# Seven more q, k and v weight chunks as three fp32r products instead of one plain fp32 product

## The chip, the cores and the metric

The kernel runs on one core of a Trainium2 chip. The metric is the device time of one execution in microseconds (us). A run of the comparison gives the median of several executions. One execution was also profiled: its rows are what the prediction rests on.

## The reference

One decoder layer over 256 tokens and 1024 channels, all in float32. A conditioning vector c gives six vectors of shift, scale and gate (adaLN). The first half of the layer is a token mixer with two groups that share one input projection:

```python
h = rms_norm(x, norm1_g) * (1 + scale1) + shift1
q, k, v, z, xbc, dt = split(h @ w_in)          # 1024, 1024, 1024, 1024, 1536, 16 columns
y_attn = rms_norm(causal_attention(rms_norm(q), rms_norm(k), v), attn_norm_g)   # 8 heads of 128
y_ssm  = group_rms_norm((ssd(silu(conv4(xbc)), dt) + x_ssm * d_skip) * silu(z), ssm_norm_g)
x = x + gate1 * (concat(y_attn, y_ssm) @ w_out)
```

The second half is a causal ConvFFN of width 2816 with its own norm, shift, scale and gate2. With 256 tokens the block-sparse attention is causal attention over one block.

## The kernel before

Weights come from memory as **chunks** of 128 partitions by up to 1024 columns, 512 KB, in one fixed order: 17 chunks of a first stage (the x, B, C, dt and a part of the z columns of the input projection), and then, counted from 0, chunks 0 to 4 (the rest of z), 5 to 20 (q and k), 21 to 28 (v), 29 to 44 (the output projection) and the FFN's. This second count is the one that the change and all texts here use. Chunks 24 and 28 have 512 columns.

Each chunk is loaded into a ring of 8 raw buffers by the loader's queue (SP, line 146), which runs in order and also issues the loads of the adaLN weight tiles (line 152, a ring of 3) and of the decay rows (line 558). A raw load waits until the chunk that used the buffer eight chunks before has given it back. A chunk is then used in one of two ways:

- **plain**: its matmuls read the raw buffer in float32, and the buffer is given back after the last of them.
- **split**: ScalarE rounds it to a hi part (line 189; GpSimd at line 187 for a few), VectorE subtracts to get the lo part (line 191), the raw buffer is given back, and every product is done as three fp32r matmuls: hi by hi, lo by hi, hi by lo, with the activations split in the same way. The hi and lo buffers are rings of five. Splits are written two chunks ahead of their use.

Which chunks are plain is a list:

```python
def plain(i):
    return i - N1 in PLAIN
...
                    if plain(c):
                        pe.matmul(bs[t], h32[:, kt, blk(t)], w[:, wc], start=(q4 == k2 == 0), stop=(kt == KT - 1))   # L806
                        continue
                    pe.matmul(bs[t], hhi[:, kt, blk(t)], w[0][:, wc], start=(q4 == k2 == 0), stop=False)   # L808
                    pe.matmul(bs[t], hhi[:, kt, blk(t)], w[1][:, wc], start=False, stop=False)             # L809
                    pe.matmul(bs[t], hlo[:, kt, blk(t)], w[0][:, wc], start=False, stop=(kt == KT - 1))    # L810
```

Between the chunks of q, k and v a table of units places other work: the convolution and softplus of the SSM group, its decay matrices (ScalarE at lines 564 to 570, VectorE at 568 to 571, products on TensorE at 582), the adaLN sums (VectorE at line 239; for one tile of this stage GpSimd at 244 with ScalarE at 248), the squares, Newton steps (lines 281 to 287), scaling (line 642) and transposes (line 648) of q and k, and then attention's scores, softmax, transposes and products. The order of each engine's instructions from the second stage on is set by a planner when the kernel is built, from the order in which they are written and from its own costs; only the loader's queue keeps the written order.

Of the kernel before, what the change touches and what calls it, by code (L numbers as in the profile page):

```python
# [21 lines left out]
NF = D_FF // 128  # L22
EPS = 1e-6
LAG = 2
PLAIN = [0, 1, 2, 3, 4, 5, 6, 8, 10, 12, 14, 16, 18, 20, 22, 24, 26, 28, 29, 30, 31, 32, 33, 34, 35, 36, 45, 46]
NEG = -1.0e30
SCALE = 128.0 ** -0.5

# [19 lines left out]
def mixer_ffn(ctx: ExitStack, tc: tile.TileContext, xT_d, c_d, vec_d, alog_d, ada_d,  # L48
# [120 lines left out]
    def plain(i):  # L169

        return i - N1 in PLAIN

# [862 lines left out]
```

## Time and profile before

| | |
|---|---|
| time, median of 3 runs | 452.51 us (451.82 to 453.27) |
| the profiled execution's own time | 452.11 us |
| its span, first to last instruction | 450.4 us |
| mean granted TensorE clock | 0.984 |
| TensorE, VectorE, ScalarE, GpSimd busy | 96%, 76%, 58%, 14% of the span |
| memory traffic | 96.71 MB, mean 215 GB/s |

The span leaves 1.7 us of the execution's time outside. PE is TensorE's matmuls and PEld its weight loads, which run beside them; DVE is VectorE, ACT ScalarE, POOL GpSimd and SPq the loader's queue. Times in rows are us from the start of the span unless they are marked ns. The granted clock is given as a share of the full clock.

### The profile page before, as it was taken

What the parts mean: (1) busy time and instruction counts of PE and PEld (TensorE: products, weight loads), DVE (VectorE), ACT (ScalarE), POOL (GpSimd) and SP (SyncE); (2) the same over time, 40 slices, a digit from 0 to 9 for tenths busy, and PEclk for the clock granted to TensorE, in tenths of its full rate; (3) what the DMA queues carried; (4) which work ended last, traced back from release to release, by engine and by line L of the source; (5) the groups of instructions that cost most, each with busy time, mean ns of one, the idle gap of its engine ahead of it and who ended that gap; (6) DMA issues with size and microseconds to landing.
All of it is one profiled execution on the core that took longest, in us unless ns stands there. A gap on an engine that the chain in (4) does not pass through costs nothing.

```text
span 450.4 us, 7730 instructions
## 1 busy us (share of the span) xinstructions
PE 433.8 (96%) x2900; PEld 384.7 (85%) x2900; DVE 344.4 (76%) x666; ACT 259.3 (58%) x523; POOL 62.3 (14%) x46
## 2 busy tenths in 40 slices
PE   7977999999999999999999989999999999999996
PEld 7876999867665566788899879999999999999996
DVE  4999992999567998647889478877777887777764
ACT  4535582945497668543237448566666665555540
POOL 3576400000000020100220000023322300000000
PEclk9789899999999999999999999999999999999999
DMA  7999674777558654245695073878677755654002
GB/s 287 399 402 400 203 239 149 255 283 268 175 175 283 229 207 182 94 141 188 222 412 206 20 307 110 282 246 258 228 254 260 234 185 186 193 174 156 0 1 95
DMA packets 31029, 96.71 MB, mean 215 GB/s; under 512 B 3712, under 2 KB 6672, under 8 KB 30992
## 3 DMA queue, kind: packets, MB, share of 16 engines
q1 hardware_dynamic: 30960, 96.20, 61.0%
q8 instruction: 23, 0.38, 0.4%
q14 instruction: 14, 0.11, 0.1%
q10 hardware_dynamic: 32, 0.02, 0.0%
HBM read 95.14 MB, written 1.06 MB: 214 GB/s over the span
## 4 chain that ended last, share of the span: by engine, by line
PE 73%; DMA 13%; DVE 7%; ACT 4%; SPq 1%; issue 1%; POOL 1%; DVEq 0%
PE bank L336 17%; PE bank L338 17%; PE bank L337 17%; PE bank L834 6%; DMA ada<-in_ada_dram 5%; PE bank L806 5%; PE bank L785 4%; DMA adax<-in_ada_dram 2%; DMA raw<-in_wv_dram 2%; DMA raw<-in_win_dram 2%; PE bank L906 1%; DVE wlo L191 1%; DMA xT<-in_xT_dram 1%; DVE ada L239 1%; DMA raw<-in_winq_dram 1%; DMA ab<-acd 1%
## 5 line engine op out<-in xcount | busy, mean ns | idle before, releaser
L191 DVE TENSOR_TENSOR wlo<-raw,whi 128x1024 fp32r<-128x1024 f32 (+3 forms) x112 | 137.4, 1235 | 15.4 <-ACT whi L189 15.0
L189 ACT ACTIVATE whi<-raw 128x1024 fp32r<-128x1024 f32 (+3 forms) x111 | 104.3, 953 | 36.7 <-PE bank L338 21.7
L336 PE MATMUL bank<-h2hi,whi 128*128 128x256 f32 x336 | 95.4, 285 | 2.1 <-ACT h2hi L876 1.9
L337 PE MATMUL bank<-h2hi,wlo 128*128 128x256 f32 x336 | 94.5, 283 | 0.0
L338 PE MATMUL bank<-h2lo,whi 128*128 128x256 f32 x336 | 93.9, 284 | 0.0
L336 PEld LDWEIGHTS bank<-h2hi,whi 128*128 128x128 f32 x336 | 64.4, 192 | 3.7 <-ACT h2hi L876 3.2
L244 POOL TENSOR_TENSOR ada<-ada,cb 128x1024 f32<-128x1024 f32 x13 | 33.4, 2569 | 241.8 <-DMA ada<-in_ada_dram 241.8
L337 PEld LDWEIGHTS bank<-h2hi,wlo 128*128 128x128 f32 x336 | 64.4, 192 | 0.0
L892 DVE SCALAR_TENSOR_TENSOR fbuf<-bank,vec,fbuf 128x255 f32<-128x255 f32 x84 | 40.4, 482 | 30.9 <-ACT fbuf L890 29.6
L338 PEld LDWEIGHTS bank<-h2lo,whi 128*128 128x128 f32 x336 | 63.8, 192 | 0.2 <-DVE h2lo L877 0.2
L336 PE MATMUL bank<-fsp,whi 128*128 128x256 f32 x176 | 49.8, 284 | 0.0
L337 PE MATMUL bank<-fsp,wlo 128*128 128x256 f32 x176 | 49.7, 283 | 0.0
L338 PE MATMUL bank<-fsp,whi 128*128 128x256 f32 x176 | 49.6, 283 | 0.0
L890 ACT ACTIVATE fbuf<-bank,vec 128x256 f32<-128x256 f32 x42 | 23.5, 561 | 36.4 <-PE bank L338 36.4
L806 PE MATMUL bank<-raw,h 128*128 128x512 f32 x96 | 44.3, 595 | 0.0
L336 PE MATMUL bank<-hhi,whi 128*128 128x256 f32 (+1 forms) x128 | 37.9, 296 | 3.7 <-DVE vS L409 2.4
L337 PE MATMUL bank<-hhi,wlo 128*128 128x256 f32 (+1 forms) x128 | 38.0, 297 | 2.2 <-DVE wlo L191 2.2
L338 PE MATMUL bank<-hlo,whi 128*128 128x256 f32 (+1 forms) x128 | 37.8, 295 | 0.7 <-DVE hlo L386 0.7
L336 PEld LDWEIGHTS bank<-fsp,whi 128*128 128x128 f32 x176 | 33.8, 192 | 0.1
L337 PEld LDWEIGHTS bank<-fsp,wlo 128*128 128x128 f32 x176 | 33.8, 192 | 0.0
L338 PEld LDWEIGHTS bank<-fsp,whi 128*128 128x128 f32 x176 | 33.7, 192 | 0.0
L239 DVE SCALAR_TENSOR_TENSOR ada<-ada,cb 128x1024 f32<-128x1024 f32 x25 | 30.3, 1216 | 3.5 <-DMA ada<-in_ada_dram 3.5
(222 smaller groups left out, 828.2 us busy)
## 6 DMA issues: line engine op xcount, KB each, us to landing
raw<-in_wup_dram SPq DMA_DIRECT2D x44, 512.0 KB, 4.2
ada<-in_ada_dram SPq DMA_DIRECT2D x38, 512.0 KB, 5.0
raw<-in_wdn_dram SPq DMA_DIRECT2D x22, 512.0 KB, 3.5
raw<-in_winq_dram SPq DMA_DIRECT2D x16, 512.0 KB, 4.3
raw<-in_wout_dram SPq DMA_DIRECT2D x16, 512.0 KB, 3.8
adax<-in_ada_dram SPq DMA_DIRECT2D x10, 512.0 KB, 7.6
raw<-in_win_dram SPq DMA_DIRECT2D x18, 256.0 KB, 7.0
raw<-in_winv_dram SPq DMA_DIRECT2D x6, 512.0 KB, 6.0
```

Of the source, the lines that this page charges most:

```text
L189: act.activation(hi[:, c], t[:, c], AF.Copy)
L191: (pool if lo_on_pool(i) else dve).tensor_tensor(lo[:, c], t[:, c], hi[:, c].bitcast(F32), op=OP.subtract)
L239: dve.scalar_tensor_tensor(t, t, 1.0, sc, op0=OP.mult, op1=OP.mult, accum_out=mod[:, i:i + 1])
L244: pool.tensor_tensor(adas[i], adas[i], sc, op=OP.mult)
L336: pe.matmul(out, w[0], h[0], start=start, stop=False, skip_group_check=True)
L337: pe.matmul(out, w[1], h[0], start=False, stop=False, skip_group_check=True)
L338: pe.matmul(out, w[0], h[1], start=False, stop=stop, skip_group_check=True)
L785: pe.matmul(zo[i], w[:, blk(kt)], h32[:, kt, 0:S], start=(kt == 0), stop=(kt == KT - 1), skip_group_check=True)
L806: pe.matmul(bs[t], h32[:, kt, blk(t)], w[:, wc], start=(q4 == k2 == 0), stop=(kt == KT - 1))
L834: pe.matmul(sacc(d), w[:, blk(kt)], X["y32"][:, kt], start=(kt == d % 2 == 0), stop=(kt == 7), skip_group_check=True)
L890: act.activation(a, src, AF.Identity, bias=vec[:, V_FB + i:V_FB + i + 1], scale=vec[:, w + 2:w + 3])
L892: dve.scalar_tensor_tensor(a[:, s:], src[:, :S - s], vec[:, w + 2 - s:w + 3 - s], a[:, s:], op0=OP.mult, op1=OP.add)
```

## The change

The list of plain chunks loses 8, 10, 12, 16, 18, 26 and 28. These seven chunks (two halves of q, two of k and the second half of v; chunk 28 is the one of 512 columns) are from then on split and done in three fp32r products. Plain remain 0 to 6, 14, 20, 22, 24, 29 to 36, 45 and 46.

```diff
-PLAIN = [0, 1, 2, 3, 4, 5, 6, 8, 10, 12, 14, 16, 18, 20, 22, 24, 26, 28, 29, 30, 31, 32, 33, 34, 35, 36, 45, 46]
+PLAIN = [0, 1, 2, 3, 4, 5, 6, 14, 20, 22, 24, 29, 30, 31, 32, 33, 34, 35, 36, 45, 46]
```

## Rows read from the trace of the kernel before

**Rows 1.** The page, part 1: engine, busy us, share of the span, instructions.

```profile
PE 433.8 (96%) x2900; PEld 384.7 (85%) x2900; DVE 344.4 (76%) x666; ACT 259.3 (58%) x523; POOL 62.3 (14%) x46
```

**Rows 2.** Busy us of each engine by stretch, granted clock, DMA share, GB/s.

```profile
core 0: us, PE busy (x) PEld busy (x) DVE busy (x) ACT busy (x) POOL busy (x), PEclk, DMA share, GB/s
...
94.00:110.00 16.00, 16.00 (x58) 9.40 (x58) 14.66 (x34) 6.06 (x15) 0.00 (x0) 1.00 0.72 268
110.00:145.00 35.00, 34.99 (x154) 21.58 (x154) 22.00 (x48) 26.39 (x79) 0.00 (x0) 1.00 0.66 207
145.00:170.00 25.00, 25.00 (x111) 14.79 (x110) 24.14 (x75) 17.89 (x61) 2.93 (x1) 1.00 0.65 232
170.00:194.50 24.50, 23.80 (x116) 17.67 (x116) 17.90 (x66) 15.89 (x50) 1.66 (x4) 1.00 0.31 112
194.50:249.00 54.50, 54.50 (x351) 50.99 (x350) 41.32 (x78) 25.93 (x49) 7.77 (x5) 1.00 0.65 242
```

**Rows 3.** TensorE's waits, 90 to 200 us: total us, times, longest.

```profile
PE bank L648 <- ACT qk L642: 0.7, 1, 0.7
```

**Rows 4.** TensorE's timeline: start, us, instruction and count (chunks 10, 11, 28).

```profile
112.57 3.59 PE L806 MATMUL bank<-raw,h 128*128 128x512 f32 x8
116.00 0.60 PE L548 MATMUL bank<-ident,xsT 128*128 128x128 f32 x4
116.36 0.48 PE L808 MATMUL bank<-whi,hhi 128*128 128x512 f32 x1
...
119.25 0.60 PE L548 MATMUL bank<-ident,xsT 128*128 128x128 f32 x4
...
191.84 1.88 PE L806 MATMUL bank<-raw,h 128*128 128x512 f32 x4
193.55 0.59 PE L699 MATMUL bank<-pT,vS 128*128 128x256 f32 x2
```

**Rows 5.** The chain of waits in order of time, two pieces of it.

```profile
116.19 0.33 SPq L146
...
116.63 4.63 DMA raw<-in_winq_dram
...
121.28 1.06 ACT whi L189
...
157.79 7.50 DMA ada<-in_ada_dram
...
165.35 2.94 POOL ada L244
...
168.31 1.15 ACT ada L248 x2
...
170.79 0.62 PE bank L648 x2
```

**Rows 6.** Waits of the loader's queue, 90 to 230 us, longest first.

```profile
SPq L146 <- PE bank L806: 58.8, 9, 9.3
```

**Rows 7.** VectorE's timeline around a lo pass, and a Newton step.

```profile
157.01 1.22 DVE L191 TENSOR_TENSOR wlo<-raw,whi 128x1024 fp32r<-128x1024 f32 x1
158.15 0.42 DVE L306 TENSOR_TENSOR accg<-accg,sq 128x256 f32<-128x256 f32 x1
...
165.99 2.31 DVE L285 TENSOR_TENSOR nw<-rqk 128x8 f32<-128x8 f32 x1
```

**Rows 8.** Timelines of VectorE and TensorE: the first decay products.

```profile
125.30 1.03 DVE L571 TENSOR_TENSOR m<-m,cbm 128x384 f32<-128x384 f32 x2 [0.95 <-ACT m L570]
...
127.53 0.66 PE L582 MATMUL bank<-m,xdt 128*64 128x256 f32 x4
```

**Rows 9.** ScalarE's timeline: evacuation of k's second half.

```profile
159.12 1.07 ACT L624 ACTIVATE qk<-bank 128x512 f32<-128x512 f32 x2
```

## The prediction

> **What bounds the kernel now.** I read the page first. TensorE is busy for 96% of the span, VectorE for 76%, ScalarE for 58% [rows 1]. A matmul that is in flight counts as busy, so the share alone proves little; the stretches and the waits have to confirm it. I then cut the span at the stages around the change. The q, k and v chunks run from about 94 us to 194.5 us. In four stretches that cover this stage TensorE is idle for 0.7 us in all, and it has its full granted clock, 1.00 [rows 2]. The view of TensorE's waits, over 90 to 200 us, has the same 0.7 us as its only row: transposes of k that wait for ScalarE [rows 3]. So the stage lasts as long as TensorE's instructions in it, and a shorter TensorE stream is worth its full length as long as nothing it consumes comes late. The stage behind it, 194.5 to 249 us, has no idle TensorE time either [rows 2]. The gain of one stage is thus handed on; I found no wait behind it that is fixed to the clock on the wall instead of to the stream.
>
> The reader should also see who is close to becoming the next bound. VectorE is busy for 14.66 of 16 us, then 22.00 of 35, then 24.14 of 25, then 17.90 of 24.5 [rows 2]. The third of these, 145 to 170 us, is full. ScalarE has 7 us free there.
>
> **What the change takes off TensorE.** Chunks 8, 10, 12, 16, 18 and 26 are full (1024 columns: 4 products of 512 columns), chunk 28 is half a chunk (2 products). In plain fp32 one product leaves two matmul records, so a full chunk is 8 of them. Chunk 10 starts at 112.57 and what follows starts at 116.00: 3.43 us, or 0.43 us a record [rows 4]. Chunk 11, the split one behind it, is 12 records of the same 512 columns. It starts at 116.36 and what follows starts at 119.25: 2.89 us, or 0.241 us a record on average, the slower first one after a plain-fp32 transpose included [rows 4]. A full chunk saves 3.43 - 2.89 = 0.54 us. Half chunk 28 takes 193.55 - 191.84 = 1.71 us plain [rows 4], and 6 x 0.241 = 1.45 us split: 0.26 us saved. Sum: 6 x 0.54 + 0.26 = 3.50 us. Against it, chunk 12 is cut up by transposes now, and each return to a split product pays the slow first record again; I take 0.1 us off: 3.4 us.
>
> [...]
>
> **What it adds.** Each full chunk gets one ScalarE copy that rounds (1.06 us for one [rows 5]) and one VectorE subtraction: the lo pass at 157.01 is followed by the next instruction at 158.15, so it holds VectorE for 1.14 us [rows 7]. Half chunk 28 takes about half of each (0.57 us by that row). ScalarE gets 6 x 1.06 + 0.53 = 6.9 us, and VectorE 6 x 1.14 + 0.57 = 7.4 us more. Between 94 and 194.5 us VectorE has 100.5 - 78.7 = 21.8 us free [rows 2], of which 3.4 us go away with the shorter stage. So 7.4 us fit into 18.4 us, and I cost them at nothing. The cover for this is TensorE's own stream and the split being made well ahead of its use. The lo pass at 157.01 is the tenth from chunk 7 on, so it is that of chunk 25, whose products run after 175 us. Where that cover is gone, at 145 to 170 us with 0.86 us free, a lo pass costs 1.14 us to whatever stands behind it; that is the slower rival. The ring of hi and lo buffers stays at five deep, which was ten chunks ahead when every other chunk was split and is now five or six, still about 15 us of TensorE's stream. I cost that at nothing too; a bound for it is one chunk's wait, 2.89 us.
>
> **What it moves.** A plain chunk gives back its raw buffer when its last matmul has ended, a split chunk when its lo pass has. The loader's queue is in order, so a raw load that waits holds up everything behind it: the loads of later chunks, the adaLN weight tiles and the loads of the decay rows (ab). Between 90 and 230 us the queue stood for 58.8 us before a raw load that waited for plain q, k, v products [rows 6]. One case is on the chain of waits: chunk 10's products end at 116.19, only then the next loads go out; a transfer that starts at 116.63 takes 4.63 us, and at 121.28 the rounding copy that waited for it runs on ScalarE, ahead of the decay work [rows 5]. With chunks 8, 10, 12, 16, 18 and 26 freed some chunks earlier, the loads of 16, 18, 20, 24, 26 and 34 go out earlier. TensorE did not wait for any of these loads, so this earns nothing by itself. But it moves the decay work forward, and that is needed: the first masked decay products end about 126.3 and TensorE takes them at 127.53 [rows 8], a slack of 1.2 us, and TensorE will come there about 1.6 us sooner (chunks 8, 10, 12). If nothing moved forward, 0.4 us would be lost there. I set 0.4 us for this and for small waits of its kind.
>
> **The sum.** 3.4 - 0.4 = 3.0 us. The profiled execution took 452.11 us; 449.1 us follows. The median shown is 452.51 us, 0.4 us above the profiled one, and an execution near the median would come to 449.5. I predict 449.3 us.
>
> **Rival one: the k chain swallows it.** The second half of k leaves TensorE just before 159.12, when ScalarE starts to evacuate it [rows 9], and comes back as transposes at 170.79 [rows 5], where TensorE already waited for 0.7 us. The way in between runs over VectorE's Newton steps, one of which took 2.31 us at 165.99 [rows 7] while a GpSimd pass ran from 165.35 to 168.29, and over ScalarE, which stood behind that pass's sum at 168.31 [rows 5]. That pass waited for an adaLN tile whose transfer took 7.50 us from 157.79. If this time stays where it is, the 2.7 us gained by chunks 8 to 18 turn into a longer stall, and only chunks 26 and 28 count: 0.54 + 0.26 = 0.8 us, 451.3 us. For it: the chain is critical now, and VectorE around it is full. Against it: its start moves with TensorE, and the adaLN tiles are behind the raw loads that come free sooner.
>
> **Rival two: slower, VectorE's queue.** If the lo passes of chunks 18, 26 and 28 or of others that the shorter ring pushes back land between 145 and 170 us ahead of k's Newton steps, three of them make the transposes 3 x 1.14 = 3.4 us later in absolute time, and the gain ahead of them is lost as well: 452.11 + 3.4 - 0.8 = 454.7 us. It decides from the point at which more than 0.86 us [rows 2] plus what moves forward is added there. For it: three lo passes are in that stretch now. Against it: 13 us of VectorE are free at 110 to 145 [rows 2], where the new passes of 10 to 18 can go, and an earlier adaLN stream moves some of its 1.2 us passes there.
>
> **Rival three: more than the forecast.** The earlier loads take the GpSimd pass and the adaLN wait off the k chain: the 0.7 us stall and my 0.4 us of small waits go, 452.11 - 3.5 - 0.7 = 447.9 us. [...]
>
> **How the numbers follow.** Forecast 0.54, with a range of its own from 448.2 to 450.6. Rival one 0.20, rival two 0.16, rival three 0.10. The smallest change that a measurement of this kernel can tell from none is about 0.3%, 1.36 us. Rival one is within it for 0.16 of its 0.20. Rival two is slower by more for 0.13, and within it for 0.03. So faster is 0.54 + 0.10 + 0.04 = 0.68, same 0.19, slower 0.13. For 8 in 10 I take 447.8, the end of rival three, to 452.8, where rival one has passed and rival two starts.
>
> **What would show it.** Right: 6 x 8 + 4 = 52 of the 96 plain records at line 806 are gone, 6 x 12 + 6 = 78 split records at lines 808 to 810 are added, each full chunk takes about 2.89 us; stage 94 to 194.5 shorter by 3 us; TensorE's waits there at most 1 us; loads and ab rows issued earlier; the later stages as long as before. Wrong: a row in TensorE's waits for ScalarE or VectorE at the k transposes or the decay products of 2 us or more (rivals one and two), or split records whose pace differs from 0.24 us.

## The result, and the profile after

The changed kernel takes 448.72 us (median of 11 executions, 447.75 to 452.04) against 452.22 us (11 executions). The ratio is 0.992, with a 95% interval of 0.9895 to 0.9946. A second comparison (the first experiment below) gave 0.9929, 0.9917 to 0.9941. By the two ratios the gain is 3.2 to 3.6 us. The forecast was 449.3 us.

The execution that was profiled first is the slowest of its eleven, 452.04 us. Its windows of the first 60 us, with those of the kernel before, show why. The columns are those of [rows 2]; the granted clock is the third number from the end.

```profile
0.00:20.00 20.00, 15.10 (x71) 14.35 (x72) 12.63 (x24) 10.06 (x17) 7.38 (x17) 0.69 0.91 341
20.00:40.00 20.00, 16.40 (x102) 14.80 (x102) 19.78 (x19) 8.99 (x15) 15.26 (x8) 0.88 1.03 400
40.00:60.00 20.00, 17.70 (x121) 16.53 (x120) 19.68 (x33) 10.55 (x21) 6.98 (x5) 0.83 0.70 241
```

```profile
0.00:20.00 20.00, 16.33 (x86) 15.50 (x87) 13.12 (x24) 10.10 (x17) 7.51 (x17) 0.83 0.88 336
20.00:40.00 20.00, 16.31 (x107) 14.30 (x105) 19.78 (x21) 10.29 (x17) 15.21 (x8) 0.91 1.03 401
40.00:60.00 20.00, 17.55 (x127) 16.75 (x128) 19.68 (x33) 10.73 (x20) 7.48 (x5) 0.91 0.72 254
```

The first fence is the changed kernel, the second the one before. TensorE was granted less of its clock (0.69, 0.88 and 0.83, against 0.83, 0.91 and 0.91), and chunk 5 starts at 97.57 us instead of 94.03. This happens ahead of everything that the change touches. I therefore compare stage by stage, and take the time of the later stages from the second profile of the changed kernel, whose execution has the usual first 60 us (0.83, 0.91, 0.91). Four lines of TensorE's timelines mark the stage, first for the kernel before, then for the second profile after: the start of chunk 5, and the first product of the attention half of the output projection.

```profile
94.03 5.31 PE L806 MATMUL bank<-raw,h 128*128 128x512 f32 x12
...
225.70 0.47 PE L336 MATMUL bank<-ahi,whi 128*128 128x256 f32 x1
```

```profile
93.92 5.31 PE L806 MATMUL bank<-raw,h 128*128 128x512 f32 x12
...
222.46 0.47 PE L336 MATMUL bank<-ahi,whi 128*128 128x256 f32 x1
```

Before it is 131.67 us, after 128.54 us (128.21 in the first profile): 3.1 to 3.5 us less, nearly the whole gain. The first split products of the FFN follow 31.58 us later before, and 31.57 us later after: what is saved in the stage is handed on.

The windows of the stage in the second profile, as [rows 2]:

```profile
94.00:110.00 16.00, 16.00 (x66) 10.64 (x65) 15.05 (x34) 7.06 (x19) 0.00 (x0) 1.00 0.92 340
110.00:145.00 35.00, 35.00 (x178) 25.40 (x177) 27.39 (x58) 28.99 (x88) 0.00 (x0) 1.00 0.62 214
145.00:170.00 25.00, 24.62 (x110) 15.53 (x109) 23.24 (x60) 21.27 (x60) 2.35 (x1) 1.00 0.57 202
170.00:190.50 20.50, 20.50 (x110) 16.51 (x108) 17.11 (x71) 12.22 (x38) 0.83 (x2) 1.00 0.34 129
```

TensorE is still busy but for 0.4 us. VectorE's additional passes went to 110 to 145 us (27.39 us busy, 22.00 before [rows 2]); 145 to 170 us is not fuller than it was (23.24 us, 24.14 before). TensorE's only wait from 90 to 200 us in the second profile, as [rows 3]:

```profile
PE bank L591 <- ACT p L674: 0.4, 1, 0.4
```

The loader's waits for plain q, k, v products there, from 90 to 228 us, as [rows 6]:

```profile
SPq L146 <- PE bank L806: 13.1, 3, 6.3
```

The wait for the k rows is gone, a smaller one for attention's exponentials has come; a second one, of 0.3 us, stands at 200.7 us. The loader waits 13.1 us instead of 58.8 us for these products. Other waits of its queue grew: for the products of the output projection (line 834) from 23.0 to 35.5 us, and for lo passes to 8.9 us.

TensorE's timeline of the first profile shows chunks 9 and 10, both split now, as [rows 4]:

```profile
112.61 0.48 PE L808 MATMUL bank<-whi,hhi 128*128 128x512 f32 x1
112.93 0.40 PE L809 MATMUL bank<-wlo,hhi 128*128 128x512 f32 x1
113.17 0.39 PE L810 MATMUL bank<-whi,hlo 128*128 128x512 f32 x1
...
115.50 0.39 PE L808 MATMUL bank<-whi,hhi 128*128 128x512 f32 x1
...
118.32 0.60 PE L548 MATMUL bank<-ident,xsT 128*128 128x128 f32 x4
```

Chunk 9, behind transposes, takes 2.89 us: its first record lasts 0.32 us to the next start, the others 0.235. Chunk 10, behind a split chunk, takes 2.82 us. In plain fp32 it took 3.43 us [rows 4].

The slow first record looks like a price of the switch from plain fp32 to split products, and the prediction charged it. It is none. Chunk 13 of the kernel before stands directly behind plain records of chunk 12:

```profile
122.91 1.88 PE L806 MATMUL bank<-raw,h 128*128 128x512 f32 x4
124.23 0.80 PE L808 MATMUL bank<-whi,hhi 128*128 128x512 f32 x1
124.87 0.39 PE L809 MATMUL bank<-wlo,hhi 128*128 128x512 f32 x1
```

Four plain records and the first split one take 1.96 us from start to start, and 4 x 0.43 + 0.235 is 1.96 as well. The split record's start is noted 0.03 us after that of the last plain record (122.91 + 3 x 0.43 = 124.20), so that it seems to last 0.64 us and the record ahead of it almost nothing. Behind transposes, which usually start 0.109 us apart, it is the same: four of them and the first split record take 0.67 us (118.32 to 118.99 in the first profile after), and 4 x 0.109 + 0.235 is 0.67. Of the 35 such switches in the second profile after, 27 add less than 0.01 us by this sum. Six stand behind decay products and add 0.2 us, as much as a plain record pays there before the change; two behind the one-column products of line 591 add 0.08 us each (the split record lasts 0.31 and 0.32 us to the next start). So a chunk that becomes split saves 3.43 - 2.82 = 0.61 us.

### The profile page after: what moved, and what is told of

It is laid out like the page before. It is cut to its first block, busy times and chain, and to the rows that moved or that the text cites. A ratio compares the mean times of both kernels' runs of the same rounds, so it can differ in the third digit from the quotient of the medians.

```text
span 450.2 us, 7801 instructions
## 1 busy us (share of the span) xinstructions
PE 433.2 (96%) x2926; PEld 392.0 (87%) x2926; DVE 351.8 (78%) x673; ACT 264.9 (59%) x530; POOL 61.9 (14%) x46
## 4 chain that ended last, share of the span: by engine, by line
PE 82%; DMA 10%; ACT 3%; DVE 3%; SPq 1%; issue 0%
PE bank L336 17%; PE bank L337 17%; PE bank L338 17%; DMA raw<-in_win_dram 6%; PE bank L834 5%; PE bank L785 4%; PE bank L808 4%; PE bank L809 4%; PE bank L810 3%; PE bank L806 3%; DMA adax<-in_ada_dram 3%; PE bank L906 1%; PE bank L582 1%; DVE wlo L191 1%; PE bank L648 1%; DMA raw<-in_wout_dram 1%
## 5 line engine op out<-in xcount | busy, mean ns | idle before, releaser
L191 DVE TENSOR_TENSOR wlo<-raw,whi 128x1024 fp32r<-128x1024 f32 (+3 forms) x119 | 141.5, 1197 | 13.6 <-ACT whi L189 13.2
L189 ACT ACTIVATE whi<-raw 128x1024 fp32r<-128x1024 f32 (+3 forms) x118 | 110.7, 953 | 37.4 <-PE bank L338 24.4
L338 PE MATMUL bank<-hlo,whi 128*128 128x256 f32 (+1 forms) x128 | 39.3, 307 | 3.3 <-DVE hlo L386 3.3
L337 PE MATMUL bank<-hhi,wlo 128*128 128x256 f32 (+1 forms) x128 | 39.0, 305 | 2.3 <-DVE wlo L191 2.3
L336 PE MATMUL bank<-hhi,whi 128*128 128x256 f32 (+1 forms) x128 | 39.1, 305 | 1.5 <-ACT hhi L380 0.9
L338 PEld LDWEIGHTS bank<-hlo,whi 128*128 128x128 f32 (+1 forms) x128 | 26.0, 203 | 4.4 <-DVE hlo L386 4.2
```

The lines of the kernel that those rows point to most:

```text
L189: act.activation(hi[:, c], t[:, c], AF.Copy)
L191: (pool if lo_on_pool(i) else dve).tensor_tensor(lo[:, c], t[:, c], hi[:, c].bitcast(F32), op=OP.subtract)
L336: pe.matmul(out, w[0], h[0], start=start, stop=False, skip_group_check=True)
L337: pe.matmul(out, w[1], h[0], start=False, stop=False, skip_group_check=True)
L338: pe.matmul(out, w[0], h[1], start=False, stop=stop, skip_group_check=True)
```

## The experiments

All times are medians beside runs of the kernel before on the same chip, with the ratio and its 95% interval. "Stage" is the stretch measured above, in the profile of that kernel (before 131.67, after 128.54 and 128.21). "Slow firsts" counts, in that stretch, the split records that follow directly on a plain-fp32 one, read from TensorE's timeline; by the sums above most of them cost nothing. SEVEN in the edits is the list of the seven chunks.

| kernel | time | ratio (interval) | stage | slow firsts |
|---|---|---|---|---|
| changed, again | 448.73 | 0.9929 (0.9917 to 0.9941) | 128.54 | 35 (before: 20) |
| passes only | 451.93 | 1.0002 (0.9986 to 1.0019) | 131.40 | 15 |
| raw buffers back early | 452.47 | 1.0007 (0.9989 to 1.0026) | 131.91 | 18 |
| changed, no lo pass | 448.94 | 0.9935 (0.992 to 0.995) | 128.42 | 42 |
| only 8 to 18 | 449.11 | 0.9928 (0.9911 to 0.9945) | 128.55 | 34 |
| changed, lo pass twice | 448.85 | 0.9926 (0.9902 to 0.9951) | 127.99 | 35 |
| all q, k, v | 448.85 | 0.9925 (0.9897 to 0.9954) | 127.92 | 41 |
| all z, q, k, v | 453.25 | 1.0041 (1.0018 to 1.0063) | 134.28 | 43 |
| only 26, 28 | 451.29 | 0.998 (0.9952 to 1.0009) | 131.45 | 23 |
| q, k, v from 7 on | 448.38 | 0.9913 (0.9886 to 0.9941) | 126.92 | 39 |
| changed, 14 and 22 too | 447.67 | 0.9901 (0.9873 to 0.9929) | 127.39 | 43 |
| changed, one product twice | 453.55 | 1.0038 (1.0018 to 1.0059) | 136.65 | 23 |

**The changed kernel again.** No edit.

> The changed kernel once more, for a second profile of it. In its first profile the stage from chunk 5 on began 3.54 us later than in the profile of before (97.57 against 94.03) because TensorE's granted clock rose later in the first 60 us, and from there to the first product of the output projection's second half it took 128.2 us against 131.7. Theory (the TensorE stream of q, k, v is shorter, nothing else): the late start is a matter of the execution and not of the change, so it may be gone or there again; the second stretch is again 3.2 to 3.7 us shorter than before, and the time is 3.0 to 4.0 us under the kernel before. Rival (the change itself delays the first stage): the late start is there again in full, about 3.5 us.

The late start is gone (chunk 5 at 93.92 us), the stage is 3.13 us shorter, and so is the time, by 0.71% of 452.29, 3.2 us. The late first stage was of that execution, not of the change.

**Is it the passes?** To the kernel before, the two passes of the seven chunks are added, and nothing else:

```diff
         if plain(i):
             ready[i] = raws.pop(i)
+            if i - N1 in SEVEN:
+                t, hi, lo = ready[i], hi_r(), lo_r()
+                for c in parts(i):
+                    act.activation(hi[:, c], t[:, c], AF.Copy)
+                    dve.tensor_tensor(lo[:, c], t[:, c], hi[:, c].bitcast(F32), op=OP.subtract)
```

> The kernel before, with the hi and lo passes of the seven chunks added on ScalarE and VectorE but their products left plain, from the raw buffer. Theory (the passes are covered by TensorE's stream): within 0.7 us of the kernel before. Rival (VectorE is the bound from 145 to 170 us): 1 to 4 us slower than before, with a wait of TensorE for the scaled k rows of 2 us or more.

Nothing is lost: 1.0002. TensorE's only wait in the stage is one of 0.8 us at the k transposes, 0.7 us before [rows 3]. So the passes are covered, in the longer stage of the kernel before.

**Is it the loads?** In the kernel before, the seven chunks are copied and their raw buffers given back at once; the products stay plain and read the copy.

```diff
+        if i - N1 in SEVEN:
+            t, hi = raws.pop(i), hi_r()
+            for c in parts(i):
+                act.activation(hi[:, c], t[:, c], AF.Copy)
+            ready[i] = hi.bitcast(F32)
+            st["split"] += 1
+            done(i)
+            return
         if plain(i):
```

> The kernel before, with the seven chunks copied by ScalarE into a hi buffer (rounded to fp32r, so the seven chunks' weights are rounded) and the raw buffer given back at once; the products stay plain, two records each, and read the copy. No lo pass. Theory (earlier loads earn nothing by themselves): within 0.7 us of the kernel before, or 0.7 us faster at most if the wait of TensorE for k goes. Rival (the gain comes from the loads and the decay work that run earlier): 2 to 3.5 us faster than before.

1.0007. The loader waits for plain q, k, v products for 21.5 us instead of 58.8, so its loads do go out earlier, and that earns nothing. TensorE's wait for k is 1.1 us there.

**Does VectorE eat a part?** In the changed kernel the lo pass of the seven is left out, or done twice:

```diff
+        if i - N1 in SEVEN:
+            t, hi = raws.pop(i), hi_r()
+            ready[i] = (hi, hi)
+            for c in parts(i):
+                act.activation(hi[:, c], t[:, c], AF.Copy)
+            st["split"] += 1
+            done(i)
+            return
         t, hi, lo = raws.pop(i), hi_r(), lo_r()
         ready[i] = (hi, lo)
```

> The changed kernel without the lo passes of the seven chunks: the second product reads the hi buffer again, so the same 78 records run and the part of lo is left out of the result. VectorE has 7.4 us less to do. Theory (the passes are covered): the same time as the changed kernel, within 0.7 us. Rival (VectorE's passes eat a part of a larger gain): 1 to 2.5 us faster than the changed kernel.

```diff
             (pool if lo_on_pool(i) else dve).tensor_tensor(lo[:, c], t[:, c], hi[:, c].bitcast(F32), op=OP.subtract)
+            if i - N1 in SEVEN:
+                dve.tensor_tensor(lo[:, c], t[:, c], hi[:, c].bitcast(F32), op=OP.subtract)
```

> The changed kernel with the lo pass of the seven chunks done twice, so VectorE has another 7.4 us in the stage, where the second profile of the changed kernel leaves it some 15 us free of 97. Theory (covered until VectorE is full): within 1 us of the changed kernel. Rival (VectorE at 145 to 170 us is already the limit): 2 to 4 us slower than the changed kernel, with TensorE waiting for VectorE there.

Neither moves the time (0.9935 and 0.9926 against 0.9929). Without the lo pass the same records run with 42 slow firsts instead of 35, and the stage is not longer for it (128.42 against 128.54), as it would be at 0.09 us each. One window from 94 to 190 us for each of three kernels: changed, lo pass twice, all q, k, v split.

```profile
94.00:190.00 96.00, 95.62 (x456) 67.77 (x454) 82.29 (x218) 69.46 (x200) 3.18 (x3) 1.00 0.60 215
```

```profile
94.00:190.00 96.00, 96.00 (x459) 68.78 (x458) 88.28 (x223) 68.34 (x199) 3.25 (x3) 1.00 0.60 214
```

```profile
94.00:190.00 96.00, 93.17 (x480) 72.16 (x479) 87.72 (x226) 72.14 (x203) 2.91 (x1) 1.00 0.63 222
```

With the lo pass twice VectorE is busy for 88.28 of 96 us and TensorE is never idle. VectorE's load alone is no limit here up to 92%.

**Which chunks give it?** Only 8, 10, 12, 16 and 18, or only 26 and 28:

```diff
-PLAIN = [0, 1, 2, 3, 4, 5, 6, 14, 20, 22, 24, 29, ...]
+PLAIN = [0, 1, 2, 3, 4, 5, 6, 14, 20, 22, 24, 26, 28, 29, ...]
```

> Only chunks 8, 10, 12, 16 and 18 are split; 26 and 28 stay plain as before. Theory (every split chunk gives its own 0.54 us): 5 x 0.54 = 2.7 us less than the kernel before, 2.2 to 3.2. Rival one of the prediction (the k chain, whose transposes come behind these chunks, swallows what they save): 0 to 0.7 us less, and TensorE's wait for the scaled k rows grows from 0.7 to about 3 us.

```diff
+PLAIN = [0, 1, 2, 3, 4, 5, 6, 8, 10, 12, 14, 16, 18, 20, 22, 24, 29, ...]
```

> Only chunks 26 and 28 are split; 8, 10, 12, 16 and 18 stay plain. Theory (every split chunk gives what its records save): 0.54 + 0.26 = 0.8 us less than the kernel before, 0.4 to 1.2. Splitting 8 to 18 alone already gave all that the change gives within the interval, so the rival is that these two give nothing: within 0.3 us of the kernel before.

The five give 0.72%, 3.3 us, just above the 2.2 to 3.2 that I expected, and the wait for k does not grow: it is gone, and TensorE waits nowhere in the stage. By their records they save 40 x 0.43 - 60 x 0.235 = 3.1 us, and the stage is 3.12 us shorter. So 26 and 28 add little to them: the stage of the changed kernel is as long as with the five alone in its second profile (128.54 and 128.55) and 0.3 us shorter in its first. The 0.9 us that their records save goes in the second profile into the two waits for attention's work, behind which TensorE's next records start 0.54 and 0.45 us late.

The two alone give 0.2%, 0.9 us, as expected, but with an interval that reaches from 2.2 us of gain to 0.4 us of loss, so their time is not settled. In their profile the stage is only 0.22 us shorter. TensorE's waits from 90 to 230 us:

```profile
PE bank L648 <- ACT qk L642: 1.3, 2, 0.8
```

12 x 0.43 - 18 x 0.235 = 0.9 us of records go, and 0.6 us more of waiting for k leave 0.3 us. Of that wait 0.5 us stand at the first half of k (156.1 us), 0.8 us at the second.

**What lies beyond the change?** More chunks split: all of q, k and v; those and z; q, k, v without 5 and 6; the changed kernel with 14 and 22.

```diff
-PLAIN = [0, 1, 2, 3, 4, 5, 6, 14, 20, 22, 24, 29, ...]
+PLAIN = [0, 1, 2, 3, 4, 29, ...]             # all q, k, v
+PLAIN = [29, ...]                            # all z, q, k, v
+PLAIN = [0, 1, 2, 3, 4, 5, 6, 29, ...]       # q, k, v from 7 on
+PLAIN = [0, 1, 2, 3, 4, 5, 6, 20, 24, 29, ...]   # 14 and 22 too
```

> All q, k and v chunks are split: 5, 6, 14, 20, 22 and the half chunk 24 too. Theory: 5 x 0.54 + 0.26 = 3.0 us more off than the change takes, about 6.4 us less than the kernel before. Rival (VectorE full): with 5.5 x 1.14 = 6.3 us more on VectorE and 3 us less time, TensorE waits for lo passes or for k, and less than 1 us more is gained, or some is lost.

> All z, q, k and v chunks are split. A plain z chunk takes about 3.45 us (16 records of 256 columns), a split one should take 24 x 0.12 = 2.9 us. Theory: 5 x 0.55 = 2.75 us more off than with z plain, about 9 us less than the kernel before. Rival (VectorE full): VectorE is busy for 13.7 of 14 us at 80 to 94 us and 14.7 of 16 us at 94 to 110; five or seven lo passes more there make the convolutions and the decay products late, TensorE waits, and the time is no better than with z plain.

> The changed kernel with 14, 20, 22 and 24 split too; 5 and 6 stay plain. In records: 28 plain ones of 0.43 us go, 42 split ones of 0.235 us come, 2.2 us, less 4 to 8 more slow first records of 0.09 us. Theory: 1.4 to 1.9 us less than the changed kernel. Rival (as with all q, k, v chunks split: what TensorE consumes comes late now, above all the decay products and the softmax): no more than 0.5 us less, with TensorE's waits in the stage at 1 us or more.

> The changed kernel with 14 and 22 split too. In records 16 x 0.43 - 24 x 0.235 = 1.2 us, less up to 8 slow first records of 0.09 us: 0.5 to 1.2 us less than the changed kernel by the theory; by the rival (consumed work comes late) nothing, with new waits of TensorE.

All q, k, v: no faster than the change. TensorE's waits from 90 to 200 us in that profile:

```profile
PE bank L582 <- DVE m L571: 1.1, 1, 1.1
PE bank L291 <- ACT p L674: 0.7, 1, 0.7
PE bank L663 <- DVE rssm L300: 0.6, 1, 0.6
PE bank L691 <- ACT p L683: 0.4, 1, 0.4
```

Against the changed kernel 44 plain records go and 66 split ones come, 18.9 - 15.5 = 3.4 us; waits of 2.8 us have come in place of the 0.4 us above, and the stage is 0.6 us shorter. The first of the waits is the decay work, whose VectorE step waited itself for its decay rows, and it had 1.2 us of slack before the change [rows 8]:

```profile
132.96 0.35 DVE L568 TENSOR_SCALAR m<-ab,nacum 128x256 f32<-128x256 f32 x1 [1.68 <-DMA ab<-acd]
133.24 1.02 DVE L571 TENSOR_TENSOR m<-m,cbm 128x384 f32<-128x384 f32 x2
...
134.31 0.66 PE L582 MATMUL bank<-m,xdt 128*64 128x256 f32 x4 [1.07 <-DVE m L571]
```

So the rival holds there, but not in the form that I wrote: over the stage VectorE is no fuller than with the lo pass twice, where nothing waits. What comes late are chains with a length of their own (the transfer of the decay rows, the softmax). The chain of waits that ends in that transfer does run over VectorE, lo passes among it, from 109.39 to 119.95 us, so VectorE's queue probably has a part in the lateness; how large it is, no run shows.

With z split as well, VectorE is full and the lo passes themselves come late. Windows, and TensorE's timeline, of that kernel:

```profile
98.00:102.00 4.00, 4.00 (x19) 3.22 (x18) 4.00 (x15) 1.27 (x4) 0.00 (x0) 1.00 0.74 262
102.00:106.00 4.00, 2.21 (x15) 1.71 (x13) 4.00 (x11) 1.17 (x2) 0.00 (x0) 1.00 0.57 208
106.00:110.00 4.00, 4.00 (x16) 2.88 (x14) 4.00 (x9) 1.14 (x4) 0.00 (x0) 0.57 1.00 343
```

```profile
105.11 0.50 PE L809 MATMUL bank<-wlo,hhi 128*128 128x512 f32 x1 [1.79 <-DVE wlo L191]
...
107.06 0.63 PE L808 MATMUL bank<-whi,hhi 128*128 128x512 f32 x1
107.49 0.63 PE L809 MATMUL bank<-wlo,hhi 128*128 128x512 f32 x1
107.92 0.63 PE L810 MATMUL bank<-whi,hlo 128*128 128x512 f32 x1
```

VectorE is busy without a gap, TensorE waits 1.79 us for a lo pass, and then its granted clock falls, to 0.57 in the window from 106 to 110 us: from 107.06 us on the records start every 0.43 us instead of 0.235. That kernel is 0.41% slower than the one before.

In between, splitting 14 and 22 has the best median, 447.67 us, and q, k, v from 7 on has 448.38. By records alone they should be 1.2 and 2.2 us below the changed kernel; the stages are 1.15 and 1.62 us shorter than in its second profile, with waits of 1.5 and 1.3 us in all instead of 0.7, and with an order that keeps every pair of decay products together (see the 3.4 us below). Their intervals overlap that of the changed kernel (0.9917 to 0.9941), so that they are faster than it is likely and not shown; both are faster than the kernel before.

**Does the stage last as long as TensorE's stream?** In the changed kernel the second product of the seven is issued twice:

```diff
+                    if c - N1 in SEVEN:
+                        pe.matmul(bs[t], hhi[:, kt, blk(t)], w[1][:, wc], start=False, stop=False)
                     pe.matmul(bs[t], hlo[:, kt, blk(t)], w[0][:, wc], start=False, stop=(kt == KT - 1))
```

> The changed kernel with the second of the three products (lo by hi) of the seven chunks done twice, so 26 more records of the same kind run and their lo part counts double in the result. Theory (the stage lasts as long as TensorE's stream): 26 x 0.235 = 6.1 us more than the changed kernel, 5.5 to 6.7, about 2.5 us more than the kernel before. Rival (TensorE has hidden waits that take up a longer stream): clearly less, 4 us more or below.

1.0038 against 0.9929 is 1.09%, 4.9 us, and by the medians 4.8 us: less than the 5.5 I set as the lower end, more than the rival's 4. A possible reason is the order of TensorE's queue: here it keeps the last pair of decay products together, which the changed kernel splits at a price of 1.2 us (see the 3.4 us below), and 6.1 - 1.2 = 4.9 us. That is an account after the fact. The profiled execution (456.5 us) is no typical one: it has waits of 1.4 us (for the exponentials) and 1.1 us (for a Newton step of k) and a granted clock of 0.91 at 170 to 190 us.

## Why the prediction held, point by point

**The bound.** Right. 44 of the 96 plain records of line 806 are left and lines 808 to 810 have 70 each instead of 44, as forecast. TensorE's stream sets the stage: the passes alone change nothing, earlier loads alone change nothing, fewer or more records change it in the direction of their sum, until something that TensorE consumes comes late. The later stages kept their length.

**The 3.4 us.** The term that was mis-sized is the charge for slow first records. Removed and added records alone are 52 x 0.43 - 78 x 0.235 = 4.0 us. My sum charged one slow first for each chunk and 0.1 us for chunk 12, about 0.6 us, for a switch that costs nothing. In its place stands a cost that I did not think of, the new order around the last two heads' decay products. Before, and then in the second profile after:

```profile
158.95 0.66 PE L582 MATMUL bank<-m,xdt 128*64 128x256 f32 x4
159.43 0.39 PE L583 MATMUL bank<-m,xdt 128*64 128x128 f32 x4
159.76 0.49 PE L663 MATMUL bank<-kT,qT 128*128 128x128 f32 x2
```

```profile
154.12 0.65 PE L582 MATMUL bank<-m,xdt 128*64 128x256 f32 x2
154.60 0.38 PE L583 MATMUL bank<-m,xdt 128*64 128x128 f32 x2
154.92 0.33 PE L648 MATMUL bank<-ident,qk 128*128 128x128 f32 x1
155.18 0.65 PE L582 MATMUL bank<-m,xdt 128*64 128x256 f32 x2
155.75 0.33 PE L648 MATMUL bank<-ident,qk 128*128 128x128 f32 x1
156.01 0.43 PE L583 MATMUL bank<-m,xdt 128*64 128x128 f32 x2
156.37 0.50 PE L808 MATMUL bank<-whi,hhi 128*128 128x512 f32 x1
```

The records of a decay product are marked 128*64, the others here 128*128. Issued together, the products of two heads run side by side: the four records of line 582 last 0.66 us and take 0.48 us to the next start before, and the two of one head alone last 0.65 us and take 0.48 us after. The planner put transposes of k between the two heads. The pair took 0.81 us before; it takes 2.25 us after, in which two transposes stand that take 0.11 us each elsewhere. That is 1.2 us more, and 2.8 us of the 4.0 are left. This price is read from the rows; no experiment changes the order of this pair alone.

**The passes at nothing.** Right, and with more room than I gave them.

**The 0.4 us of small waits.** Wrong as a sum: waits did not grow. The decay work moved with TensorE. In the first profile after:

```profile
127.64 1.03 DVE L571 TENSOR_TENSOR m<-m,cbm 128x384 f32<-128x384 f32 x2 [1.82 <-ACT m L570]
...
129.02 0.66 PE L582 MATMUL bank<-m,xdt 128*64 128x256 f32 x4
```

Counted from the start of chunk 5, the products come 31.45 us after it instead of 33.50, their factors are ready at 31.10 instead of 32.30 [rows 8]. The slack shrank from 1.2 to 0.35 us and held. The 0.7 us at k went, 0.3 to 0.7 us of other waits came. So the net of 3.0 us that I forecast came out of errors that cancel, and that it lies so near is in part luck: 0.6 us too little from the records, nothing for the split pair of decay products (1.2 us), and 0.4 us too much for waits. Records and that pair explain 2.8 us of the 3.1 to 3.5; the other 0.3 to 0.7 us lie in waits and in the transposes of k (three of them took 0.75 us at 155.78 us before, against 0.11 us each elsewhere), and I don't assign them further.

**Rival one, k swallows it.** Fell, in a way that I had not thought of. I held the place of the k transposes in TensorE's queue fixed. The planner put them later, among the products of chunk 25 instead of 23. In the first profile after:

```profile
176.94 0.39 PE L808 MATMUL bank<-whi,hhi 128*128 128x512 f32 x1
177.17 0.27 PE L648 MATMUL bank<-ident,qk 128*128 128x128 f32 x1
```

They come 79.6 us after chunk 5, 76.8 us before the change [rows 5], and TensorE fills the time with products of v and with scores. Of the runs that split 8 to 18, only the one with a product twice shows a stall at k, 1.1 us for its Newton step; with only 26 and 28 split the wait at the second half of k is 0.8 us, against 0.7 before. That the new order is what avoided the stall is argued from these profiles: no run holds the order fixed.

**Rival two, VectorE's queue.** Fell for the change, since the passes found room at 110 to 145 us. Its signs appear with z split too, at 98 to 110 us.

**Rival three, more.** The wait at k did go, as it said, but not by earlier loads: giving the buffers back early left a wait of 1.1 us there. Nor did the records get faster: the split ones of 512 columns keep 0.235 us from start to start, before and after.

## What to carry to other kernels

Take a price from start to start over everything around the instruction, never from one record: a first record that looked 0.09 us slower cost nothing, because the record ahead of it looked as much shorter. Then look at what the new order does to the other work of the busiest engine: two groups of products that ran side by side and were pulled apart took back 1.2 of 4.0 us here. Where a planner sets the order, a wait at one place is not fixed: ask what the engine could do meanwhile. As the busiest engine's stream gets shorter, the next bound need not be the second busiest engine; it can be a chain with little slack (1.2 us at the decay products here), and that slack can be read from the trace beforehand.

## What was not expected of the hardware

With z split too, a single wait of TensorE of 1.79 us, which ended at 105.11 us, was followed by a lower clock: 0.57 granted from 106 to 110 us, and 1.00 in the windows of 4 us before and behind. My estimate is about 3.4 us at half the clock: 0.43 of it is missing over 4 us, 0.50 is what was granted from 10 to 15 us in the profile before and in the first one after, and 4 x 0.43 / 0.5 = 3.4. Between the end of the wait and the slow records, 105.11 to 107.06 us, TensorE's records follow each other without a wait. Two executions of the changed kernel reached chunk 5 at 97.57 and at 93.92 us, by nothing else that I could see than the clock granted in the first 60 us (0.69, 0.88 and 0.83 against 0.83, 0.91 and 0.91).
